# Layer 0's MLP in two phases, with sums in PSUM and activations through DRAM, in a two-layer encoder on one Trainium2 core

## The chip, the cores and the metric

The kernel runs as one program on one core of a Trainium2 chip. The metric is device time in microseconds (us) of that core. Three executions of the kernel before took 2149.87, 2150.5 and 2151.79 us, median 2150.5.

## The reference

256 tokens of width 2048 pass two layers. Each layer is modulated by a vector `c`; the part that matters here is the MLP:

```
for l in range(2):
    mod = silu(c) @ w_ada[l] + b_ada[l]          # six vectors of 2048: sh_a, sc_a, g_a, sh_m, sc_m, g_m
    h = rmsnorm(x) * (1 + sc_a) + sh_a
    ...                                          # two kinds of attention, x += g_a * mix
    h = rmsnorm(x) * (1 + sc_m) + sh_m
    y = square(relu(h @ w_mlp_in[l])) @ w_mlp_out[l]     # 2048 -> 8192 -> 2048
    x = x + g_m * y
return rmsnorm(x, final_norm_g)
```

All is float32. The products with weights are computed with each operand in two reduced-precision parts, high and low ("hi", "lo"): hi by hi, hi by lo and lo by hi.

## The kernel before, in words

**Weights.** `weights` (L167, L170) loads 1 MB by SyncE (SP) into one of five `raw` buffers; ScalarE (ACT) copies the hi part, VectorE (DVE) subtracts for the lo part, each in two halves of 1024 columns. Four hi and four lo halves fit. A `raw` buffer is free again when its lo is done. SP issues its transfers in one order that is fixed when the program is built; the order on each engine comes from a planner, except that TensorE in the MLPs keeps program order (`manual_schedule`).

**Ada.** The product `silu(c) @ w_ada` does not go to TensorE. Each of its 192 blocks is a 1 MB load into a `raw` buffer and one DVE multiply with a running sum (L323; one block of the 192 goes another way). The blocks are spread over the kernel: each call of `weights` earns a credit of `self.rate`, and each whole credit issues one ada load, whose DVE product is placed behind the splits of a later call. `ada_need` forces what is not there in time. When a pair of blocks is summed, its two columns of `mod` are written (L334, L336).

**First product of the MLP.** `wides` takes two tiles of 128 of the 8192 columns at a time: for 16 slices of the width, hi weights stand in TensorE and the hi and lo activations pass (512 columns, L232), then the lo weights and hi activations (256 columns, L235). In layer 0 the first 12 tiles are computed while the norm is applied, so 52 tiles, 26 pairs, are left for `mlp`.

**Second product, layer 0 (`mlp`).** The 8192 columns are taken in four blocks of 2048. After 16 tiles of a block, `rows` (L1325, L1327, L1329) multiplies them: the activations stand, 512 columns of weights pass, three matmuls for each of 16 slices, two token halves and four groups of 512 output columns. Each block's sums leave PSUM: copied for the first block, added to `y` by DVE for the other three (L1025). In the last block the output groups are finished one after the other, `turned` transposes finished ones and adds them to `x`, and `ahead` starts layer 1's input product.

**Second product, layer 1 (`mlp_last`).** The 8192 columns are 32 pairs of tiles. Output columns 0 to 1023 are summed in PSUM over all 32 pairs while the first product still runs (phase 1, four pairs behind it). A pair's activations, 2 by 2 blocks with the 2 by 2 blocks of its weights, can be multiplied in eight block products of three matmuls, 24 matmuls (`eight`), or in seven (`products`, 21 matmuls), after additions on the weights (`seven_weights`, L1155 to L1166) and on the activations (`sums4`). The parts of the activations (28 pairs) and of their sums are written to DRAM (`spill`) and read again (`fetch`, the tile `back`). Phase 2 then does output columns 1024 to 2047 for the first 24 pairs (13 by `eight`, 11 by `products`), and `rows` does the last 8 pairs in two groups of 512 columns (`c` = 2, 3). `leave` copies the seven-product banks out (L1215) and `gather` adds them up.

**The end.** `end_tile` finishes 512 output columns of a token half: times `g_m` (L1279), plus `x` (L1280), square with row sum (L1265), times the norm's weight; for the last group the root and reciprocal follow, and `end` scales the rows (L1299, L1301, L1303) and writes them out (L1307).

**Pools.** The activations `h`, `hid`, `y` and `back` share one pool `up` of 40 tiles of 256 KB; the additions' hi and lo parts in `seven_weights` have a pool `kp` that exists in layer 1's MLP only; PSUM has eight banks.

Of the kernel before, what the change touches and what calls it, by code (L numbers as in the profile page):

```python
# [26 lines left out]
NFB = DFF // D  # L27
# [73 lines left out]
ORDER = 1, 2, 3, 5, 7, 6, 4  # L101

# [3 lines left out]
RATE_A0, RATE_Q, RATE_A3, RATE_O, RATE_A1, RATE_A2, RATE_K, RATE_M, RATE_V = 0.7, 2.7, 1.7, 0.75, 0.5, 0.7, 0.6, 0.68, 1.4  # L106
# [3 lines left out]
class Trunk:  # L110
    def __init__(self, ctx, tc, io):
# [4 lines left out]
        self.up = pool("up", 40)  # L116
# [7 lines left out]
        self.ap = self.late.enter_context(tc.tile_pool(name="ap", bufs=6))  # L124
# [20 lines left out]
    def u(self, name, dt=F32):  # L145
        return self.up.tile([P, 2, T], dt, tag="u", name=self.name(name))
# [40 lines left out]
    def parts(self, name):  # L187

        v = self.u(name, F32R)
        return v[:, 0], v[:, 1], v.rearrange("p a b -> p (a b)")  # L190
# [125 lines left out]
    def ada_sums(self, after=None):  # L316
# [4 lines left out]
        for w, l, g, i in now:  # L321
            acc = self.macc[l, g]
            ins = nc.vector.scalar_tensor_tensor(  # L323
                w, w, 1.0, self.cond, ALU.mult, ALU.mult, accum_out=acc[:, i : i + 1]
            )
            self.summed = ins
            if after is not None:
                self.follow(ins, after)
            if i % 2:
                c = slice(i - 1, i + 1)  # L330
                v = V_BADA + 96 * l + NK * g + i
                b = self.vec[:, v - 1 : v + 1]
# [20 lines left out]
    def ada_need(self, l, g, i, after=None):  # L353
        most = self.most
# [279 lines left out]
    def ahead_rest(self, st, first, acc, after, loads=0):  # L634

        h = []
        for p in range(first, 8):
# [7 lines left out]
            if p >= after:  # L645
                upto = NK if p == 7 else 2 * (p - after + 1)
                while len(h) < upto:
                    h += self.modulated(r, len(h), self.mod[st.l, st.sh], self.mod[st.l, st.sc], after=self.lo)
# [13 lines left out]
    def modulated(self, r, k, sh, sc, whole=None, after=None, scaled=False):  # L662
# [3 lines left out]
        out = [self.parts("h") for _ in range(2)]  # L666
# [45 lines left out]
    def norm_then_by_k(self, l, acc, sh, sc, src, n, nwhole, fill=(), early=()):  # L712
# [5 lines left out]
        for p in range(8):  # L718
# [10 lines left out]
            h += self.modulated(of, k, self.mod[l, sh], self.mod[l, sc], whole, self.lo if p - 1 in early else None, not sh or p == 0)  # L729
# [26 lines left out]
    def layer(self, l, acc, st):  # L756
# [190 lines left out]
        with self.tc.manual_schedule(engines={mybir.EngineType.PE}) if l else nullcontext():  # L947
# [23 lines left out]
            else:  # L971
                h, banks = self.norm_then_by_k(l, acc, 3, 4, io["w_n0"], 3, 0)
                high = self.high
                first = NNORM, lambda: [
                    self.relu2(b, after=a) for b, a in zip(banks, [high, *self.highs, *self.highs[1:] * 3])
                ]
# [4 lines left out]
    def mlp(self, l, h, first, g):  # L981
        io = self.io
        done, leave = first
        y = [[None] * 4 for _ in range(2)]
        acc = None
        nxt = self.ahead(l + 1, 0, 1, io["w_a1"][0])
        held = []
        for fb in range(NFB):
            hid = []
            for m in range(0 if fb else done, NK, 2):  # L990
                pss = self.wides([io["w_m1"][l, NK * fb + m + j - NAHEAD] for j in range(2)], h)
                if leave:
                    hid += sum(leave(), [])
                    leave = None
                    held = [pss]
                    continue
                for ps in held + [pss]:
                    hid += self.relu2(self.joined(ps, self.t("sum")))
                held = []
            last = fb == NFB - 1  # L1000
            for cols in ((0, 1), (2,), (3,)) if last else ((0, 1), (2, 3)):
                n = len(cols)
                todo = ()
                if last:
                    self.ada_need(l, 5, NK - 1)
                    todo = (0, 1) if cols == (2,) else (2,) if cols == (3,) else ()
                pss = [[self.bank("py") for _ in range(2)] for _ in cols]
                steps = 8 * n // 2
                for kp in range(steps):
                    w = self.weights(io["w_m2"][l, fb, cols[0] // 2, (cols[0] % 2) * 4 + kp])  # L1010
                    self.rows(pss, w, hid[kp * NK // steps : (kp + 1) * NK // steps], kp == 0, kp == steps - 1)
                    if todo and kp == 1:
                        for c in todo:
                            acc = self.turned(c, y, g, acc, nxt)
                if cols == (3,):
                    self.rate = 0.0
                    self.ahead_step(nxt, 0)
                for c, ps in zip(cols, pss):
                    for t in range(2):
                        flat = ps[t].rearrange("p a b -> p (a b)")  # L1020
                        if fb == 0:
                            y[t][c] = self.u("y").rearrange("p a b -> p (a b)")
                            self.nc.scalar.activation(y[t][c], flat, AF.Copy)
                        else:
                            self.nc.vector.tensor_tensor(y[t][c], flat, y[t][c], ALU.add)  # L1025
        acc = self.turned(3, y, g, acc, nxt)
        return self.ahead_rest(nxt, 1, acc, 2, 7), nxt

    def mlp_last(self, l, h, first, g):
        io, tc = self.io, self.tc  # L1030
        done, leave = first
        self.ada_need(l, 5, NK - 1)
        self.late.close()
        self.kp = self.late.enter_context(tc.tile_pool(name="kp", bufs=1))
        self.dp = self.late.enter_context(tc.tile_pool(name="dp", bufs=1, space=bass.MemoryType.DRAM))
        hid, part, kept = {}, {}, {}
        sevens = range(3, NSPLIT, 2)
# [3 lines left out]
        def own(j, v, bias=None):  # L1041
            hid[j] = self.hidden(v, bias)
            if j < NPAIR - LAG:
                kept[j] = self.spill(hid[j], f"a{j}")

        def sums(j, v):
            part[j] = self.sums4(v)
            if j in sevens:
                kept[j] += self.spill(part[j], f"s{j}")

        for j in range(lead, NPAIR):
            pre = [self.t("pre") for _ in range(2)]
            step = j - LAG
            for i in range(2):
# [12 lines left out]
                if i == 0:  # L1067
                    banks = banks or {p: self.flat(self.bank("p7")) for p in ORDER}
                    w = self.seven_weights(io["w_s"][0, step])
# [4 lines left out]
        for j in range(NPAIR - LAG, NPAIR):  # L1074
            if (NPAIR - j) % 2:
                self.products(banks, ORDER, self.seven_weights(io["w_s"][0, j]), hid[j], part[j], False, j == NPAIR - 1)
            else:
                self.eight(banks, self.weights(io["w_s"][0, j]), hid[j], (0,) if j == NPAIR - LAG else (), j == NPAIR - 2)
        first = self.leave(banks)
        banks = {p: self.flat(self.bank("p8")) for p in (0, *ORDER)}  # L1080
        for j in range(NSPLIT):
            if j == 4:
                y = self.gather(first)
            a = self.fetch(kept[j][:2])
            if j in sevens:
                p = self.fetch(kept[j][2:])
                self.products(banks, ORDER, self.seven_weights(io["w_s"][1, j]), a, p, j == 3, j == NSPLIT - 1, (2, 3, 4))
            else:
                self.eight(banks, self.weights(io["w_s"][1, j]), a, (0, 2, 3, 4) if j == 0 else (), j == NSPLIT - 2)
        y = [a + b for a, b in zip(y, self.gather(self.leave(banks)))]  # L1090
        late, hid = hid, []
        for j in range(NSPLIT, NPAIR):
            hi, lo = self.fetch(kept[j]) if j in kept else late[j]
            hid += [(hi[:, i], lo[:, i], None) for i in range(2)]
        rows, turn, done = self.end_plan(y, g)
        work = {2: {1: [rows(2)], 2: [rows(3), turn(2)], 3: [turn(3)]}, 3: {0: [rows(0), rows(1)], 1: [turn(0), done(0)], 2: [turn(1), done(1)]}}
        for c in (2, 3):
            pss = [[self.bank("py") for _ in range(2)]]
            for kp in range(4):
                w = self.weights(io["w_e"][0, c - 2, kp])  # L1100
                self.rows(pss, w, hid[kp * 4 : kp * 4 + 4], kp == 0, kp == 3, c == 3 and kp == 3)
                for f in work[c].get(kp, ()):
                    f()
            for t in range(2):
                self.before = self.end_tile(y[t][c], self.flat(pss[0][t]), c, t)
        return y, None

# [3 lines left out]
    def hidden(self, v, bias=None):  # L1111

        nc = self.nc
        r = v
        if bias is None:
            nc.scalar.activation(r, v, AF.Relu)
# [4 lines left out]
        return self.both(r, self.u("hidl", F32R), "hidh")  # L1121

    def sums4(self, r):
# [6 lines left out]
        return self.both(s.rearrange("p (a b) c -> p a (b c)", a=2), self.u("suml", F32R), "sumh")  # L1130
# [55 lines left out]
    def eight(self, banks, w, a, first, last):  # L1186
# [3 lines left out]
        for p, t, c in ((0, 1, 1), (2, 0, 0), (3, 0, 1), (4, 1, 0)):  # L1190
            for k in range(2):
                self.product(banks[p], x(k, t), n(k, c), p in first and k == 0, last and p == 0 and k == 1)
# [25 lines left out]
    def end_plan(self, y, g):  # L1218
# [30 lines left out]
        def done(c):  # L1249
            def f():  # L1250
                for t in range(2):
                    self.end_square(y[t][c], c, t)
# [10 lines left out]
    def end_square(self, z, c, t):  # L1263
        sq = self.flat(self.t("zsq"))
        self.nc.scalar.activation(sq, z, AF.Square, accum_out=self.part[:, c, t : t + 1])  # L1265
# [6 lines left out]
    def end_tile(self, z, ps, c, t):  # L1272

        nc = self.nc
        flat = lambda v: v.rearrange("p a b -> p (a b)")
        m, zf = flat(self.t("zm")), z
        if c == 3 and t == 0:
            zf = self.y3 = flat(self.u("zf"))
        nc.vector.tensor_tensor(m, ps, self.gb[c], ALU.mult)  # L1279
        last = nc.vector.tensor_tensor(z, m, z, ALU.add)  # L1280
        self.end_square(z, c, t)
        if c < 3 or t == 0:
# [405 lines left out]
```

## Time and profile before

| | |
|---|---|
| median of three executions | 2150.5 us |
| profiled execution, its own time | 2150.3 us |
| its span in the profile | 2148.5 us |
| mean granted clock of TensorE | 0.997 |
| HBM read, written | 602.81 MB, 22.54 MB |

How to read it: lines L... are those of the kernel before. A row of a group gives line, engine, operation, output tile <- input tiles, shapes and count, then the busy time in us, the mean of one in ns, and the idle time of the engine ahead of it with what ended it. "PE" is a matmul, "PEld" a weight load that overlaps it. Matmuls overlap, so the duration of one (about 390 ns for 512 columns) is more than the distance from one to the next. The chain is the sequence of work that ended last, followed back from the end. In layer 0's MLP the first `wides` begins at 474.9 us and the last matmul of `rows` at 1114 us; layer 1's phase 2 is about 1967 to 2090 us.

### The profile page before, as it was taken

The page shows a single profiled execution, that of the slowest core. Times are in us where ns is not written, and L with a number is a line of the kernel's source. Part 1 is how long each engine was busy: PE and PEld are TensorE (multiplying, and loading weights), DVE is VectorE, ACT ScalarE, POOL GpSimd, SP SyncE. Part 2 cuts the span into 40 slices and gives each one's busy share as a digit, 9 for nine tenths or more (in the row PEclk, how much of TensorE's full clock was granted, in tenths as well). Part 3 has the DMA queues.
Part 4 walks back from the last instruction along what each step waited for, and adds up shares of the span by engine and source line. Part 5 has one row for each costly group of instructions (what it writes and reads, how often), then busy time and mean ns, then how long its engine had stood idle before and what let it go on. Part 6 is the DMA issues. An engine that isn't in the chain of part 4 may idle for free.

```text
span 2148.5 us, 30886 instructions
## 1 busy us (share of the span) xinstructions
PE 2127.4 (99%) x11925; PEld 1866.4 (87%) x11925; DVE 1809.8 (84%) x2336; ACT 1244.1 (58%) x1937; POOL 24.7 (1%) x43
## 2 busy tenths in 40 slices
PE   8999999999999999999999999999999999999998
PEld 6899888998888888888889898989888888888886
DVE  8999988888687778778798788798998888888887
ACT  6555664555455355345447656647767666665554
POOL 0000000000000000000001000000000000000000
PEclk9999999999999999999999999999999999999999
DMA  9987988799888888888877657786776766758993
GB/s 399 424 329 263 342 331 291 264 377 332 320 319 325 332 296 337 328 309 318 333 251 259 249 198 294 274 299 208 268 268 237 263 250 231 263 193 303 356 332 115
DMA packets 108006, 627.38 MB, mean 292 GB/s; under 512 B 11985, under 2 KB 11985, under 8 KB 41809
## 3 DMA queue, kind: packets, MB, share of 16 engines
q1 hardware_dynamic: 107570, 624.75, 77.7%
q8 instruction: 94, 1.54, 0.3%
q10 hardware_dynamic: 288, 0.66, 0.1%
q14 instruction: 54, 0.44, 0.1%
HBM read 602.81 MB, written 22.54 MB: 291 GB/s over the span
## 4 chain that ended last, share of the span: by engine, by line
PE 92%; DVE 3%; ACT 3%; DMA 2%; issue 0%; DVEq 0%; ACTq 0%
PE ps L232 24%; PE ps L235 13%; PE py L1327 6%; PE py L1325 6%; PE py L1329 6%; PE p L1174 4%; PE p L1175 4%; PE p L1176 4%; PE pk L262 3%; PE pk L210 2%; PE pk L208 2%; PE pk L209 2%; PE pv L276 1%; PE pv L278 1%; PE pv L277 1%; DVE lo L170 1%
## 5 line engine op out<-in xcount | busy, mean ns | idle before, releaser
L170 DVE TENSOR_TENSOR lo<-raw,hi 128x1024 fp32r<-128x1024 f32 (+1 forms) x638 | 746.1, 1190 | 222.3 <-ACT hi L167 152.3
L167 ACT ACTIVATE hi<-raw 128x1024 fp32r<-128x1024 f32 (+1 forms) x638 | 645.3, 1031 | 448.5 <-PE py L1329 186.1
L232 PE MATMUL ps<-h,hi 128*128 128x512 f32 x2016 | 475.1, 390 | 0.0
L232 PEld LDWEIGHTS ps<-h,hi 128*128 128x128 f32 x2016 | 376.3, 188 | 77.0 <-ACT hi L167 0.2
L323 DVE SCALAR_TENSOR_TENSOR ada<-ada,cond 128x2048 f32<-128x2048 f32 x191 | 434.7, 2283 | 3.1 <-DMA ada<-in_w_ada 2.9
L235 PEld LDWEIGHTS ps<-h,lo 128*128 128x128 f32 x2016 | 254.2, 191 | 7.6 <-DVE lo L170 0.4
L235 PE MATMUL ps<-h,lo 128*128 128x256 f32 x2016 | 256.6, 283 | 0.2 <-DVE lo L170 0.2
L1325 PE MATMUL py<-hi,hid 128*128 128x512 f32 x512 | 163.0, 390 | 0.0
L1327 PE MATMUL py<-lo,hid 128*128 128x512 f32 x512 | 163.0, 389 | 0.0
L1329 PE MATMUL py<-hi,hid 128*128 128x512 f32 x512 | 162.9, 389 | 0.0
L1327 PEld LDWEIGHTS py<-lo,hid 128*128 128x128 f32 x512 | 96.1, 188 | 20.3 <-DVE lo L170 0.4
L1329 PEld LDWEIGHTS py<-hi,hid 128*128 128x128 f32 x512 | 96.1, 188 | 20.0
L1325 PEld LDWEIGHTS py<-hi,hid 128*128 128x128 f32 x512 | 95.8, 188 | 19.6
L1166 DVE TENSOR_TENSOR ul<-u,uh 128x2048 fp32r<-128x2048 f32 x41 | 93.9, 2291 | 15.5 <-ACT uh L1165 12.8
L1165 ACT ACTIVATE dh<-raw 128x1024 fp32r<-128x1024 f32 x82 | 65.1, 841 | 67.4 <-PE p L1176 57.2
L1060 ACT ACTIVATE pre<-ps 128x256 f32<-128x256 f32 x116 | 37.9, 379 | 101.4 <-PE ps L235 101.4
L1165 ACT ACTIVATE uh<-u 128x1024 fp32r<-128x1024 f32 x82 | 85.7, 1055 | 11.8 <-issue 10.5
L208 PE MATMUL pk<-h,hi 128*128 128x256 f32 x304 | 85.4, 287 | 2.2 <-ACT h L673 1.5
L209 PE MATMUL pk<-h,hi 128*128 128x256 f32 x304 | 86.2, 286 | 0.0
L210 PE MATMUL pk<-h,lo 128*128 128x256 f32 x304 | 85.2, 287 | 0.3 <-DVE lo L170 0.2
L1166 DVE TENSOR_TENSOR dl<-raw,dh 128x1536 fp32r<-128x1536 f32 x41 | 71.8, 1752 | 6.6 <-ACT dh L1165 6.6
L262 PE MATMUL pk<-hf,w 128*128 128x256 f32 x288 | 63.1, 379 | 0.0
(393 smaller groups left out, 3830.2 us busy)
## 6 DMA issues: line engine op xcount, KB each, us to landing
ada<-in_w_ada SPq DMA_DIRECT2D x191, 1024.0 KB, 5.2
raw<-in_w_m SPq DMA_DIRECT2D x174, 1024.0 KB, 5.6
raw<-in_w_s SPq DMA_DIRECT2D x56, 1024.0 KB, 6.4
raw<-in_w_ob SPq DMA_DIRECT2D x24, 1024.0 KB, 5.0
raw<-in_w_dv SPq DMA_DIRECT2D x16, 1024.0 KB, 5.2
raw<-in_w_q SPq DMA_DIRECT2D x16, 1024.0 KB, 5.0
back<-a SPq DMA_DIRECT2D x56, 256.0 KB, 6.8
raw<-in_w_n SPq DMA_DIRECT2D x16, 768.0 KB, 5.9
```

The source lines that it names most:

```text
L167: ins = self.high = nc.scalar.activation(hi, v, AF.Copy)
L170: ins = nc.vector.tensor_tensor(lo, v, hi.bitcast(F32), ALU.subtract)
L208: mm(ps, hi, x[0], start=first, stop=False, skip_group_check=shared)
L209: mm(ps, hi, x[1], start=False, stop=False, skip_group_check=shared)
L232: mm(ps.rearrange("p a b -> p (a b)"), part(w, 0, k), both, start=k == 0, stop=False)
L235: mm(ps[:, 0], part(w, 1, k), x, start=False, stop=k == nk - 1)
L323: ins = nc.vector.scalar_tensor_tensor(w, w, 1.0, self.cond, ALU.mult, ALU.mult, accum_out=acc[:, i : i + 1])
L1165: nc.scalar.activation(hi[:, c:m], v[:, c:m], AF.Copy)
L1166: nc.vector.tensor_tensor(lo, v, hi.bitcast(F32), ALU.subtract)
L1325: mm(o, xh[:, tok], hi[:, part[j]], start=start, stop=False)
L1327: mm(o, xh[:, tok], lo[:, part[j]], start=False, stop=False)
L1329: mm(o, xl[:, tok], hi[:, part[j]], start=False, stop=stop)
```

## The change

Layer 0's `mlp` takes the form of layer 1's, with one difference: its phase 1 uses `eight` alone, so that the four sums for columns 0 to 1023 take four banks and two pairs of `wides` fit beside them. Each round of phase 1 is one pair of `wides` and one plain step (two in the three rounds behind the first). Phase 2 is shared by both layers (`second`): steps 3, 5, ... 23 by `products`, the others by `eight`. The last 8 pairs go through `rows` with single groups of 512 columns.

The pool `up` shrinks from 40 to 32 tiles; 8 tiles of a pool `xp` hold the later half of the attention's `h`, layer 0's first four activations and the sums. `kp` for layer 0 takes the place of `xp` and of the pool of `ahead` while phase 2 runs. Rates: `RATE_M` 0.68 to 0.76, `RATE_A1` 0.5 to 0.6, `RATE_A2` 0.7 to 0.9, new `RATE_S` 0.2 for phase 2 and `RATE_E` 0.75 for the last 8 pairs. `mod` is written for eight blocks at once, except layer 0's shifts and scales.

At the end of layer 1, the last group's later two weight loads are multiplied for token half 0 first, then half 1; of half 1, the last load's sums go to two banks of 256 columns each, which are finished one after the other, and the norm's weight is multiplied in ahead of the reciprocal.

```diff
     def mlp(self, l, h, first, g):
...
+        for j in range(lead, NPAIR):
+            pss = self.wides([io["w_m1"][l, 2 * j + i - NAHEAD] for i in range(2)], h)
+            if j == lead:
+                for k, (ps, after) in enumerate(leave()):
+                    own(k, ps, r=self.t("relu"), after=after, far=k < 4)
+            pre = [self.t("pre") for _ in range(2)]
+            for i, ps in enumerate(pss):
+                for k in range(2):
+                    nc.scalar.activation(pre[k][:, i], ps[:, k], AF.Copy)
+            nc.vector.tensor_tensor(pre[0], pre[0], pre[1], ALU.add)
+            own(j, pre[0])
+            for _ in range(2 if j > lead else 0):
+                if step <= j - LAG:
+                    banks = banks or {p: self.flat(self.bank("p4")) for p in PLAIN}
+                    self.eight(banks, self.weights(io["w_s"][2 * l, step]), hid[step], PLAIN if step == 0 else (), ())
+                    step += 1
+        for j in range(step, NPAIR):
+            self.eight(banks, self.weights(io["w_s"][2 * l, j]), hid[j], (), PLAIN if j == NPAIR - 1 else ())
+        self.rate = RATE_S
...
+        banks = self.second(l, kept)
+        for t, v in enumerate(self.gather(self.leave(banks))):
+            y[t][2:] = v
...
+        hid = self.rest(hid, kept)
+        self.rate = RATE_E
...
+        for c in (2, 3):
+            ps = [self.bank("py") for _ in range(2)]
+            for kp in range(4):
+                w = self.weights(io["w_e"][l, c - 2, kp])
+                self.rows([ps], w, hid[4 * kp : 4 * kp + 4], kp == 0, kp == 3)
...
+    def second(self, l, kept, then=None):
+        banks = {p: self.flat(self.bank("p8")) for p in (*PLAIN, *(p for p in ORDER if p not in PLAIN))}
+        for j in range(NSPLIT):
+            if then is not None and j == 4:
+                then()
+            a = self.fetch(kept[j][:2])
+            w = self.io["w_s"][2 * l + 1, j]
+            if j in SEVENS:
+                p = self.fetch(kept[j][2:])
+                self.products(banks, ORDER, self.seven_weights(w), a, p, j == SEVENS[0], j == SEVENS[-1], PLAIN)
+            else:
+                self.eight(banks, self.weights(w), a, PLAIN if j == 0 else (), (0,) if j == NSPLIT - 2 else ())
+        return banks
...
     def mlp_last(self, l, h, first, g):
...
+        for t in range(2):
+            for n, (x, w) in enumerate(ws if t == 0 else ws[:4]):
+                self.product(ps[t], self.token(x, t), w, False, n == (3 if t else 7))
+            if t == 0:
+                self.end_last(y[0][3], ps[:1], 0, (slice(0, 512),))
+                continue
+            self.end_add(y[1][3], ps[1], 3)
+            halves = slice(0, 256), slice(256, 512)
+            ps = [self.flat(self.bank("pz")) for _ in halves]
+            for p, c in zip(ps, halves):
+                for n, (x, w) in enumerate(ws[4:]):
+                    self.product(p[:, c], self.token(x, t), [z[:, c] for z in w], n == 0, n == 3)
+            self.end_last(y[1][3], ps, 1, halves)
...
+    def end_last(self, z, ps, t, cols):
+        m = self.flat(self.u("zf"))
+        some = self.some[:, t : t + 1]
+        for i, c in enumerate(cols):
+            self.end_add(z, ps[i], 3, c)          # times g_m, plus z
+            sq = self.s("zq", 1)
+            self.end_square(z[:, c], sq)
+            nc.vector.tensor_tensor(m[:, c], z[:, c], self.fgb[3][:, c], ALU.mult)
...
+        r = self.s("rt", 1)
+        nc.scalar.activation(r, sq, AF.Sqrt, bias=some, scale=INV_D)
+        nc.vector.reciprocal(r, r)
```

More of the change, by code (lines that the diff above doesn't have):

```diff
@@ L981, in mlp @@
     def mlp(self, l, h, first, g):
-        io = self.io
+        io, nc = self.io, self.nc
         done, leave = first
-        y = [[None] * 4 for _ in range(2)]
-        acc = None
[L986 to L1004, printed above, removed]
-                    self.ada_need(l, 5, NK - 1)
[L1006 to L1025, printed above, removed]
@@ new lines, in mlp, with own @@
+        nxt = self.ahead(l + 1, 0, 1, io["w_a1"][0])
+        hid, kept = {}, {}
+        lead, step, banks = done // 2, 0, None
+        def own(j, v, **k):
+            hid[j] = self.hidden(v, **k)
+            if j < NPAIR - LAG:
+                kept[j] = self.spill(hid[j], f"a{l}{j}")
+            if j in SEVENS:
+                kept[j] += self.spill(self.sums4(k.get("r", v)), f"s{l}{j}")
+        for j in range(lead, NPAIR):
[14 more added lines that the diff above has]
+                    step += 1
@@ L1029, in mlp_last, with rest @@
+    def rest(self, hid, kept):
+        out = []
+        for j in range(NSPLIT, NPAIR):
+            hi, lo = self.fetch(kept[j]) if j in kept else hid[j]
+            out += [(hi[:, i], lo[:, i], None) for i in range(2)]
+        return out
     def mlp_last(self, l, h, first, g):
@@ L1079, in mlp_last @@
         first = self.leave(banks)
[L1080 to L1089, printed above, removed]
+        y = []
@@ L1090, in mlp_last @@
+        banks = self.second(l, kept, lambda: y.extend(self.gather(first)))
         y = [a + b for a, b in zip(y, self.gather(self.leave(banks)))]
[L1091 to L1094, printed above, removed]
+        hid = self.rest(hid, kept)
         rows, turn, done = self.end_plan(y, g)
-        work = {2: {1: [rows(2)], 2: [rows(3), turn(2)], 3: [turn(3)]}, 3: {0: [rows(0), rows(1)], 1: [turn(0), done(0)], 2: [turn(1), done(1)]}}
+        work = {2: {1: [rows(2)], 2: [rows(3), turn(2)], 3: [turn(3)]}, 3: {0: [rows(0), rows(1), turn(0), done(0)], 1: [turn(1), done(1)]}}
@@ L1191, in eight @@
             for k in range(2):
-                self.product(banks[p], x(k, t), n(k, c), p in first and k == 0, last and p == 0 and k == 1)
+                self.product(banks[p], x(k, t), n(k, c), p in first and k == 0, p in last and k == 1)
     def leave(self, banks):
@@ L1369, in joined @@
         return out
-    def relu2(self, ps, bias=None, after=None):
-        r = self.t("relu")
-        if bias is None:
-            ins = self.nc.scalar.activation(r, ps, AF.Relu)
-            if after is not None:
-                self.follow(ins, after)
-        else:
-            for i in range(2):
-                self.nc.scalar.activation(r[:, i], ps[:, i], AF.Relu, bias=bias[:, i : i + 1])
-        self.nc.scalar.activation(r, r, AF.Square)
-        return self.split(r, "hid", True)
     def rope_k(self, ps, l):
```

174 lines of the change are left out of this document (93 added, 81 removed).

## The prediction

> **What bounds the kernel now.** I read the page's busy table first, then the chain in layer 0's MLP, then windows by stage, then the groups.
>
> ```profile
> span 2148.5 us, 30886 instructions
> PE 2127.4 (99%) x11925; PEld 1866.4 (87%) x11925; DVE 1809.8 (84%) x2336; ACT 1244.1 (58%) x1937; POOL 24.7 (1%) x43
> ```
> TensorE is busy almost always, but a busy PE need not be at its peak, so I take its pitch. First the chain across one change from the first product to the second in layer 0 (start, us, what):
> ```profile
> 661.92 7.28 PE ps L232 x32
> 669.20 3.83 PE ps L235 x32
> 673.04 0.47 PE py L1325 x2
> ```
> A pair of first-product tiles takes 7.28 + 3.83 = 11.11 us, a 256-column matmul 3.83/32 = 0.120, and the second product starts without a gap. The pitch of a 512-column matmul, from the end of layer 1's second phase (48 matmuls from the first row to the second):
> ```profile
> 2079.61 0.39 PE L1174 MATMUL p<-uh,back 128*128 128x512 f32 x1
> ...
> 2090.27 0.39 PE L1176 MATMUL p<-uh,back 128*128 128x512 f32 x1
> ```
> (2090.27 - 2079.61)/47 = 0.227 us. Layer 0's second product:
> ```profile
> L1325 PE MATMUL py<-hi,hid 128*128 128x512 f32 x512 | 163.0, 390 | 0.0
> ```
> L1327 and L1329 have as many: 1536. 26 pairs by 11.11 plus 1536 by 0.227 is 288.9 + 348.4 = 637 us. So here matmuls removed are time removed, while what feeds TensorE keeps up. What feeds it, by windows (PE, PEld, DVE, ACT, POOL busy, clock, DMA share, GB/s):
> ```profile
> 584.00:760.00 176.00, 176.00 (x898) 150.88 (x897) 138.52 (x157) 89.01 (x116) 6.55 (x6) 1.00 0.86 323
> 1518.00:1700.00 182.00, 182.00 (x976) 157.86 (x975) 164.03 (x183) 125.74 (x188) 0.00 (x0) 1.00 0.68 254
> 1966.00:2090.00 124.00, 124.00 (x547) 102.35 (x546) 102.51 (x88) 66.69 (x78) 0.00 (x0) 1.00 0.94 355
> 60.00:70.00 10.00, 10.00 (x48) 8.59 (x47) 9.05 (x15) 7.08 (x14) 0.00 (x0) 1.00 1.03 427
> 1970.00:1980.00 10.00, 10.00 (x46) 8.28 (x45) 9.83 (x11) 4.71 (x5) 0.00 (x0) 1.00 1.04 408
> ```
> First row: layer 0's MLP now (DVE 79%, 323 GB/s). Second and third: layer 1's two phases, the form that layer 0 is to take; TensorE stands still in neither, with DVE at 90% or DMA at 355 GB/s. The last two: the DMA engines saturated, 427 GB/s with loads alone, 408 with small fetches among them.
>
> **The change, step by step.**
>
> *Second product.* Phase 1 gives columns 0 to 1023 to 32 plain steps of 24 matmuls (768, as before). Phase 2 has 13 plain steps and 11 of 21, 543; the rest 8 loads of 24, 192. Sum 1503, 33 fewer: 33 by 0.227 = 7.5 us, on the path. First product, transposes and the lead into layer 1 keep their counts.
>
> *DVE.* Per split and ada product of layer 0, and per step of layer 1:
> ```profile
> L170 DVE TENSOR_TENSOR lo<-raw,hi 128x1024 fp32r<-128x1024 f32 x231 | 277.1, 1220 | 120.2 <-ACT hi L167 75.2 <-issue 22.1 <-PE ps L235 17.3
> L323 DVE SCALAR_TENSOR_TENSOR ada<-ada,cond 128x2048 f32<-128x2048 f32 x79 | 180.3, 2282 | 0.0
> L202 DVE TENSOR_TENSOR hid<-relu,hid 128x256 fp32r<-128x256 f32 x64 | 24.0, 418 | 5.4 <-ACT hid L201 5.4
> L1366 DVE TENSOR_TENSOR sum<-ps,sum 128x256 f32<-128x256 f32 x52 | 21.5, 417 | 0.0
> ```
> ```profile
> L1166 DVE TENSOR_TENSOR ul<-u,uh 128x2048 fp32r<-128x2048 f32 x40 | 91.6, 2291 | 14.9 <-ACT uh L1165 12.2
> L1166 DVE TENSOR_TENSOR dl<-raw,dh 128x1536 fp32r<-128x1536 f32 x40 | 70.1, 1751 | 6.6 <-ACT dh L1165 6.6
> L1155 DVE TENSOR_TENSOR u<-raw 128x1024 f32<-128x1024 f32 x40 | 48.7, 1217 | 1.2 <-DMA raw<-in_w_s 1.2
> L1157 DVE TENSOR_TENSOR u<-u,raw 128x512 f32<-128x512 f32 x40 | 27.6, 690 | 1.1
> L1156 DVE TENSOR_TENSOR u<-u,raw 128x512 f32<-128x512 f32 x40 | 27.4, 685 | 0.3
> L1416 DVE TENSOR_TENSOR suml<-sum,sumh 128x512 fp32r<-128x512 f32 x29 | 19.9, 685 | 0.2
> L1416 DVE TENSOR_TENSOR hidl<-pre,hidh 128x512 fp32r<-128x512 f32 x28 | 19.1, 684 | 0.4 <-ACT hidh L1415 0.4
> ```
> A seven-product weight costs DVE 6.6 us against 2.4 for two plain splits, per step of 21 by 0.227 = 4.8 us. Phase 2 sums to 13 by 2.4 + 11 by 6.6 = 104 us and 2.6 ada products (13 loads at rate 0.2) 6: 110 of its 123 us, 90%. In phase 1 one round (a pair and a plain step, 11.11 + 5.44 = 16.6 us) has six splits 7.3, 2.28 ada products 5.3, joining and splitting the activation 1.4, and sums in 11 of 26 rounds about 0.7: 14.7 us, 89%. Both are at what layer 1 bears unharmed, so I cost them at nothing; cover gone, phase 2's 6 us of ada is the price. ACT trades 256-wide copies for 512-wide ones and splits the combined weights; it is busy 89 of 176 us now and would have to double to be seen. The mod sums go out in eights instead of pairs, fewer small DVE operations: idle time either way.
>
> *DMA, all on SP's queue.* Weights stay 116 loads. Ada loads go from 79 (the count above) to 84 by 0.76 + 13 by 0.2 + 8 by 0.75 = 72; the 7 left go to layer 1's attention, whose rates rise (17 loads by 0.1 and 16 by 0.2 more, 5) and whose last ada is due when its MLP begins; one or two loads forced there would cost 2.3 us of DVE each (the L323 row), beside TensorE's first products. New are spills and fetches, as in layer 1 (out<-in, KB each, us to landing; a weight load, then the fetches):
> ```profile
> raw<-in_w_s SPq DMA_DIRECT2D x56, 1024.0 KB, 6.4
> ```
> ```profile
> back<-a SPq DMA_DIRECT2D x49, 256.0 KB, 6.9
> back<-s SPq DMA_DIRECT2D x22, 256.0 KB, 6.2
> ```
> Written are 28 pairs and 11 sums by 0.52 MB, 20.4 MB, and as much read. With 188 loads of 1.05 MB the MLP moves 238 MB in 632 us: 377 GB/s, phase 1 379, phase 2 375, against 323 now. That lies between the 355 that ran with a DMA share of 0.94 and the 408 of saturation; nearer to neither. I take it as borne, because what is served at 408 is the same mix, and keep the other end for the range. A spill that waits for its activation holds the weight loads behind it on SP; the five raw buffers cover it, and layer 1 issues the same order.
>
> The Trainium skill, "DMA: Bandwidth & Descriptors", section "Where 436 GB/s comes from", has HBM traffic bound by about 358 GB/s per core, and its measured single-core load near 425. By the former, an estimate, the MLP would need 238/358 = 665 us, 33 more; the 427 row above speaks for the latter.
>
> *The junction in each round.* Both forms of weights share four hi and four lo buffers. A pair takes all four lo; the plain step behind it needs its two lo 0.2 and 0.9 us after the pair ends at 11.1, and their buffers come free at 7.28 + 0.96 = 8.2 and 9.2 us. Before, this stood four times in the MLP, now in 25 rounds. DVE there, before:
> ```profile
> 670.25 2.36 DVE L170 TENSOR_TENSOR lo<-raw,hi 128x1024 fp32r<-128x1024 f32 x2 [2.99 <-issue]
> ```
> The two splits end at 672.61, 0.4 us before the pair does and 1.3 before the second would be needed, after idle time that a DVE at 89% won't always have. An ada product of 2.3 us begun just before 8.2 ends at 10.5 and puts the splits to 11.7 and 12.9, 0.4 and 0.9 us late: the price is 0 to 25 by 0.9 = 22 us. The junctions of before cost 0, and the order on DVE must fall badly for the other end; near the lower one I take 0.05 each, +1.3 us.
>
> *Pools and banks.* The activation pool falls from 40 to 32 with 8 apart; at the worst (16 h, 6 pairs of activations) 28 are live, so nothing waits that did not. Between the phases of layer 0 four banks are copied out by ACT:
> ```profile
> L1215 ACT ACTIVATE y<-p 128x512 f32<-128x512 f32 x16 | 8.8, 603 | 2.7 <-PE p L1176 2.5
> ```
> Phase 2 starts on the banks of the finished first product and asks for the copied ones in its fourth step, 3 by 5.4 = 16 us later, against 4 by 0.6 = 2.4 us: nothing, and 2.4 us if the cover is gone. Its combined weights overlay the far pool, whose last user is step 23's sums, eight steps before.
>
> *The end.* The last matmul, and what follows it on DVE, the chain (zsq, final product) and SP:
> ```profile
> 2139.21 0.39 PE L1329 MATMUL py<-hi,hidl 128*128 128x512 f32 x1
> ```
> ```profile
> 2139.63 0.69 DVE L1279 TENSOR_TENSOR zm<-py,gb 128x512 f32<-128x512 f32 x1
> 2140.36 0.69 DVE L1280 TENSOR_TENSOR y<-zm,y 128x512 f32<-128x512 f32 x1
> ```
> ```profile
> 2141.08 0.73 ACT zsq L1265 x2
> ...
> 2143.24 0.66 DVE y L1301
> ```
> ```profile
> 2142.61 2.51 SPq L1307 DMA_DIRECT2D out_y<-y  x4
> ```
> From 2139.6 to the end are 8.9 us. On half the width zm and y take 0.42 each (L1366), 0.54 less, the square about 0.2 less, and the last product becomes a plain scaling of 0.48 (2143.24's row has 0.66): about 0.9. SP now issues four outputs in a burst and its last leaves at 2145.12, 1.2 after the last product; after, token half 0's four go out while half 1 still multiplies, so up to 1 us more. PE pays 24 by 0.120 for 12 by 0.227: +0.15. I take -1.7 net, bounds -2.6 and +0.5 (half 0's scalings ahead of half 1 on DVE).
>
> **Sum**, on the profiled execution's 2150.3 us (0.2 below the median 2150.5): 2150.3 - 7.5 - 1.7 + 1.3 = 2142.4.
>
> **Rivals.** *A, DMA becomes the bound in layer 0's MLP* (slower): loads land late in SP's order, an ada product waits on DVE and the splits behind it with it. It decides where the sustained rate falls under 238/(632 + 9) = 371 GB/s; at 365 the MLP takes 652, 20 more: 2150.3 - 9.2 + 20 = 2161. For it: 355 at share 0.94 makes 378 a full share, and 89% DVE at once; against: 408 and 427. 17%. The page's 358 is its far end.
> *B, the junction costs 0.35 us in each round* (no change): +8.8 in place of 1.3, 2150. For it the 1.3 us of margin, less than one ada product; against, the gapless ones of before. 13%.
> *C, phase 2's ada and one handover show*, 4 us beyond the forecast: 2146. For it 110 of 123 us on DVE; against, layer 1's phase 2 without a gap. 8%.
>
> **How the numbers follow.** Forecast 62%, own range 2139 to 2146. 0.2%, about what a measurement here tells from no change, is 4.3 us. Faster: the forecast and half of C, 0.66; same: the rest of C and most of B, 0.16; slower: A and some of B, 0.18. The range runs from 2139.5 (tail's best, no junction loss) to 2154, into A.
>
> **What would show it.** 33 fewer 512-column matmuls in the MLP; each round 16.6 us long; PE idle under 2 us there; DMA 370 to 380 GB/s; the end 7 us behind the last matmul. Wrong if a round's plain step begins late behind lo (B), if DVE's ada shows idle time on DMA (A), or if phase 2 takes over 125 us (C).

## The result, and the profile after

The changed kernel takes 2210.1 us (median of four, 2204.3 to 2216.5) for 2150.2 (four, 2147.7 to 2151.8) in the same session: a ratio of 1.028, 95% interval 1.0245 to 1.0316. It is slower by 60 us where 8 us less were forecast. The profiled execution took 2205.9. Its page:

```profile
span 2204.1 us, 31205 instructions
PE 2139.4 (97%) x11904; PEld 1863.3 (85%) x11904; DVE 1857.2 (84%) x2302; ACT 1273.8 (58%) x1996; POOL 18.2 (1%) x43
```

TensorE has fewer matmuls than before (11904 for 11925) and is idle for 65 us instead of 21. Where: the first and last matmul of layer 1's input product (`pa`) frame the stages, first of the kernel before, then of the changed one, with the changed one's second phase (`back`, first start) beside it.

```profile
L209 PE MATMUL pa<-al,hi x192: 277/282/295, 1114.9 to 1489.9; 128*128 128x258 f32 x192
```
```profile
L213 PE MATMUL pa<-al,hi x192: 277/282/419, 1164.3 to 1545.3; 128*128 128x258 f32 x192
```
```profile
L1227 PE MATMUL p<-hi,back x208: 389/389/397, 991.9 to 2141.5; 128*128 128x512 f32 x104
```

Up to the end of layer 0's MLP 49.4 us are lost, in layer 1's attention 381.0 - 375.0 = 6.0, from there to the end 0.2. The MLP by windows (columns as in the prediction), before and after:

```profile
474.00:981.00 507.00, 507.00 (x2571) 434.05 (x2570) 399.37 (x454) 257.52 (x341) 6.55 (x6) 1.00 0.86 323
```
```profile
474.00:981.00 507.00, 468.95 (x2385) 392.87 (x2384) 383.31 (x398) 254.19 (x370) 0.00 (x0) 0.98 0.88 341
981.00:1104.00 123.00, 123.00 (x544) 101.72 (x543) 104.30 (x88) 67.07 (x74) 0.00 (x0) 1.00 0.99 382
```

The loss is in phase 1: from 474 to 991.9, 518 us where 26 pairs by 11.11 and 768 matmuls by 0.227 make 463. TensorE is idle there, the DMA engines move 341 GB/s of the 379 needed, and no engine is full. Phase 2 runs as forecast, at 382 GB/s. What TensorE waited for in phase 1 (us in total, times, longest), and what SP's queue waited for at its head:

```profile
PE ps L236 <- ACT hi L171: 20.5, 9, 8.4
PE p L1228 <- DVE lo L174: 11.3, 17, 0.8
PE p L1227 <- ACT hi L171: 5.6, 5, 1.7
```
```profile
SPq L1189 <- ACT hidh L1466: 171.8, 22, 10.1
```

L1189 is `spill`. One such wait in SP's order of time (start, duration, issue):

```profile
687.20 0.43 SPq L188 DMA_DIRECT2D raw<-in_w_m  x1
687.72 0.58 SPq L317 DMA_DIRECT2D ada<-in_w_ada  x1
696.34 0.33 SPq L1189 DMA_DIRECT2D a<-hidh  x1
698.30 0.33 SPq L1189 DMA_DIRECT2D a<-hidl  x1
698.72 0.38 SPq L188 DMA_DIRECT2D raw<-in_w_m  x1
```

For 8 us nothing is issued; the next pair's second load (698.72) stands behind a spill that waits for the pair now being multiplied. At the end of that pair, ACT:

```profile
690.19 0.66 ACT L1007 ACTIVATE pre<-ps 128x256 f32<-128x256 f32 x2 [6.06 <-PE ps L239]
691.40 1.06 ACT L171 ACTIVATE hi<-raw 128x1024 fp32r<-128x1024 f32 x1 [0.55 <-DMA raw<-in_w_s]
692.37 0.64 ACT L1007 ACTIVATE pre<-ps 128x256 f32<-128x256 f32 x2
692.89 1.06 ACT L171 ACTIVATE hi<-raw 128x1024 fp32r<-128x1024 f32 x1
```

The plain step's first hi stands behind the first tile's two copies and waits for its load, the second behind all four copies. So hi and lo are late when the pair has ended: here TensorE stops 0.44 us for hi and 0.76 and 0.78 us for lo, the kind of stop in the second and third row of its waits. The order on ACT is not the same in every round; one round earlier only two copies stand ahead of the second hi.

### The profile page after: what moved, and what is told of

Same layout as the page of the kernel before. It is cut to its first block, busy times and chain, and to the rows that moved or that the text cites. A ratio compares the mean times of both kernels' runs of the same rounds, so it can differ in the third digit from the quotient of the medians.

```text
span 2204.1 us, 31205 instructions
## 1 busy us (share of the span) xinstructions
PE 2139.4 (97%) x11904; PEld 1863.3 (85%) x11904; DVE 1857.2 (84%) x2302; ACT 1273.8 (58%) x1996; POOL 18.2 (1%) x43
## 4 chain that ended last, share of the span: by engine, by line
PE 79%; DVE 9%; DMA 5%; ACT 5%; issue 2%; SPq 0%; DVEq 0%; ACTq 0%
PE ps L236 21%; PE ps L239 11%; PE p L1228 8%; PE p L1229 8%; PE p L1227 8%; DVE lo L174 3%; PE pk L266 3%; DVE ada L327 3%; DMA raw<-in_w_m 2%; ACT hi L171 2%; PE pv L281 1%; PE pv L282 1%; PE pv L280 1%; PE pk L212 1%; PE pk L213 1%
## 5 line engine op out<-in xcount | busy, mean ns | idle before, releaser
L174 DVE TENSOR_TENSOR lo<-raw,hi 128x1024 fp32r<-128x1024 f32 (+1 forms) x616 | 719.0, 1190 | 204.0 <-ACT hi L171 158.4
L171 ACT ACTIVATE hi<-raw 128x1024 fp32r<-128x1024 f32 (+1 forms) x616 | 617.5, 1029 | 358.6 <-DMA raw<-in_w_m 51.2
L1219 DVE TENSOR_TENSOR ul<-u,uh 128x2048 fp32r<-128x2048 f32 x52 | 119.2, 2292 | 27.2 <-ACT uh L1218 24.6
L1218 ACT ACTIVATE uh<-u 128x1024 fp32r<-128x1024 f32 x104 | 109.0, 1057 | 43.2 <-DVE u L1210 18.5
L1228 PE MATMUL p<-lo,hidh 128*128 128x512 f32 x272 | 109.9, 404 | 11.9 <-DVE lo L174 11.3
L1227 PE MATMUL p<-hi,hidh 128*128 128x512 f32 x272 | 108.3, 398 | 5.6 <-ACT hi L171 5.6
L1229 PE MATMUL p<-hi,hidl 128*128 128x512 f32 x272 | 107.2, 394 | 0.0
L1104 ACT ACTIVATE pre<-ps 128x256 f32<-128x256 f32 x116 | 37.9, 379 | 100.5 <-PE ps L239 100.4
L1007 ACT ACTIVATE pre<-ps 128x256 f32<-128x256 f32 x104 | 34.3, 380 | 99.1 <-PE ps L239 99.0
L1229 PE MATMUL p<-hi,back 128*128 128x512 f32 x208 | 81.0, 389 | 0.0
L1228 PE MATMUL p<-lo,back 128*128 128x512 f32 x208 | 80.9, 389 | 0.0
L1227 PE MATMUL p<-hi,back 128*128 128x512 f32 x208 | 80.9, 389 | 0.0
```

Of the source, the lines that this page charges most:

```text
L171: ins = self.high = nc.scalar.activation(hi, v, AF.Copy)
L174: ins = nc.vector.tensor_tensor(lo, v, hi.bitcast(F32), ALU.subtract)
L1218: nc.scalar.activation(hi[:, c:m], v[:, c:m], AF.Copy)
L1219: nc.vector.tensor_tensor(lo, v, hi.bitcast(F32), ALU.subtract)
L1227: mm(ps, x[0], w[0], start=first, stop=False)
L1228: mm(ps, x[0], w[1], start=False, stop=False)
```

## The experiments

Three theories. ORDER: a spill that waits at the head of SP's queue holds the loads behind it. BYTES: the DMA engines can't carry phase 1 (rival A). JUNCTION: the plain step's lo is late behind each pair (rival B). Times of single runs unless said; the kernel before took 2148 to 2155 beside them. The changed kernel's own four runs lie up to 12 us apart, so a smaller difference from it is no evidence by itself.

**Spills on GpSimd's queue**
```
-            self.nc.sync.dma_start(d, v.bitcast(F32))
+            q = self.nc.gpsimd if name[1] == '0' else self.nc.sync
+            q.dma_start(d, v.bitcast(F32))
```


> Layer 0's spills are issued by GpSimd's queue in place of SP's; bytes, waits and everything else as in the changed kernel. Theory ORDER (a spill waits at the head of SP's queue for its activations and the weight loads behind it start late): phase 1 of layer 0 goes from 518 us to under 475, the run to 2146-2162 us. Theory BYTES (the DMA engines cannot carry weights, ada, spills at once): phase 1 stays over 505, the run at 2200-2216. Theory JUNCTION (DVE's lo splits are late behind each pair): the matmuls' waits for DVE's lo of 11 us stay and the run stays over 2195.

2161.3 us, 45 less, as ORDER has it. Window of phase 1 (it ends at 945.6) and TensorE's waits in it:
```profile
474.00:945.00 471.00, 465.20 (x2422) 399.51 (x2421) 384.81 (x402) 256.36 (x374) 40.11 (x74) 0.99 0.97 374
```
```profile
PE ps L236 <- ACT hi L171: 5.1, 2, 3.4
PE p L1229 <- DVE lo L174: 0.5, 2, 0.3
```
The same bytes at 374 GB/s, so BYTES is out. But two things have changed: the planner, which orders the engines when the program is built, now puts the plain step's two hi ahead of the pair's copies:
```profile
678.77 2.01 ACT L171 ACTIVATE hi<-raw 128x1024 fp32r<-128x1024 f32 x2 [0.45 <-DMA raw<-in_w_s]
684.49 0.66 ACT L1007 ACTIVATE pre<-ps 128x256 f32<-128x256 f32 x2 [3.71 <-PE ps L239]
686.41 0.66 ACT L1007 ACTIVATE pre<-ps 128x256 f32<-128x256 f32 x2 [1.26 <-PE ps L239]
```

**Spills on SP that are ready at once** (they write a slice of `x`, not the activation)
```
+            v = self.x[:, 2 * i : 2 * i + 2] if name[1] == '0' else v.bitcast(F32)
```


> Layer 0's spills stay on SP and keep their number and bytes, but write a slice of x, which is ready long before, in place of the activations (what phase 2 reads back of layer 0 is therefore not the activations). ORDER: no spill waits, phase 1 under 475 us, the run 2146-2162. BYTES: the same bytes, phase 1 over 505, the run 2200-2216. JUNCTION: over 2195.

2189.9, outside all the forecasts. SP has no spill waits left, but ACT's order is the late one and TensorE waits 19 times, 12.7 us, for lo. ORDER alone doesn't carry the 55 us.

**Spills a sixteenth in size, in their places on SP** (the other columns are not written)
```
+                self.nc.sync.dma_start(d, v[:, :, :16].bitcast(F32))
```


> Layer 0's spills keep their waits and their places on SP but write 16 of 256 columns, a sixteenth of the bytes (only the first pair is written whole, and phase 2 reads that pair for all). ORDER: the loads are held as before, phase 1 500-518 us, the run 2190-2206. BYTES: 20 MB less in phase 1, so it falls under 480 and the run to 2146-2170. JUNCTION: over 2195.

2199.4, as ORDER has it: without 15/16 of the bytes it is 6.5 us less, within the spread of the changed kernel, and SP still waits 176.6 us for `hidh`. A second answer against BYTES.

**Each spill issued one round later in the program**
```
-                kept[j] = self.spill(hid[j], f"a{l}{j}")
+                wait.append((j, hid[j], f"a{l}{j}"))     # issued behind the next pair's loads
```


> Layer 0's spills stay on SP, but each is issued one round later in the program, behind the next round's pair. ORDER: most waits at SP's head vanish, phase 1 465-490 us, the run 2150-2178. BYTES: phase 1 over 505, the run 2200-2216. JUNCTION: over 2195.

2206.8, no gain. The waits for `hidh` fell to 30.6 us, those for `sumh` are 29.6, and waits for a free `raw` buffer rose from 61 and 17 us to 130 and 70; TensorE waits 22 times for lo. A miss.

**The plain step's weights requested ahead of the pair's copies, spills on SP**
```
+            ws = [self.weights(io["w_s"][2 * l, step + i]) for i in range(n)]
             pre = [self.t("pre") for _ in range(2)]
```


> The changed kernel, with the plain step's two weights requested in the program ahead of the pair's activation copies and spill in each of layer 0's rounds; the spills stay on SP. So on SP two loads go out before each waiting spill, and on ACT and DVE the weights' hi and lo come before the copies that wait for the end of the pair. JUNCTION in its new form (the second hi stands behind two copies that wait for the pair, 0.7 us a round in 25 rounds, and the clock lost after each of those stops): 16 to 25 us less than the changed kernel's 2206, 2181 to 2190, and the waits of the plain step's products for lo go to nearly 0. ORDER alone (a spill that waits for its activation holds whatever loads stand behind it, wherever they stand): the pair's loads of the next round are still behind the spill, so most of the loss stays, 2195 to 2206. If both are cured by this order alone: 2155 to 2170.

2207.9, no gain: the planner mixed both orders over the rounds, and the spills kept their place ahead of the next pair's loads.

**ACT's order forced, three ways.** First, GpSimd spills with the plain step's second hi behind all four copies (in every round; in the changed kernel two or four copies stand ahead of it, so that the expectation's "as it stands" is too kind):
```
+                    copied = nc.scalar.activation(pre[k][:, i], ps[:, k], AF.Copy)
...
+                    self.eight(banks, self.weights(io["w_s"][2 * l, step], after=copied, first=1), ...)
```


> Spills on GpSimd's queue (2161.3 us), and on ACT the second hi of every plain step in layer 0's first phase is put behind the pair's four copies, as it stands in the changed kernel. JUNCTION: each round's plain step then waits for lo, 0.5 to 0.9 us in 25 rounds, and the clock is lost behind each stop as in the kernel with ready spills: 2161 + 12 to 28 = 2173 to 2189. ORDER alone: within 4 us of 2161, since the loads come as early as before.

2253.1, 92 us more: far beyond either forecast. One round of TensorE:
```profile
714.61 0.39 PE L1230 MATMUL p<-hi,hidl 128*128 128x512 f32 x1
716.00 0.49 PE L1228 MATMUL p<-hi,hidh 128*128 128x512 f32 x1 [1.00 <-ACT hi L171]
717.26 0.50 PE L1229 MATMUL p<-lo,hidh 128*128 128x512 f32 x1 [0.77 <-DVE lo L174]
...
718.60 0.63 PE L1228 MATMUL p<-hi,hidh 128*128 128x512 f32 x1
719.03 0.63 PE L1229 MATMUL p<-lo,hidh 128*128 128x512 f32 x1
...
721.59 0.51 PE L1229 MATMUL p<-lo,hidh 128*128 128x512 f32 x1
```
```profile
594.69:602.69 8.00, 7.23 (x31) 5.76 (x32) 8.00 (x12) 5.94 (x8) 1.62 (x3) 1.00 0.74 224
716.00:724.00 8.00, 7.24 (x24) 5.55 (x24) 7.20 (x10) 4.34 (x6) 1.08 (x2) 0.79 0.75 270
718.60:721.60 3.00, 3.00 (x9) 2.31 (x8) 3.00 (x6) 0.80 (x2) 0.83 (x2) 0.50 0.81 337
754.00:794.00 40.00, 36.47 (x170) 29.83 (x169) 28.37 (x30) 17.48 (x26) 3.25 (x6) 0.91 0.80 297
```
The two stops lose 1.39 + 1.26 - 2 by 0.227 = 2.2 us. Then seven matmuls from 718.60 take (721.59 - 718.60)/7 = 0.427 us each instead of 0.227, with the granted clock at 0.50: another 1.6 us or so. The two stops come in all 25 rounds, the low clock in the last 20 of them; in the first five (the row from 594.69 is the fifth) the same stops leave it at 1.00. 25 by 2.2 + 20 by 1.6 = 87 of the 92 us. The prediction bounded the junction's price by the wait alone; with the clock it is 3.9 us a round. The Trainium skill, "TensorE: Matmul & The Clock Gate", section "HAM oscillation — how this bites in real kernels", has the clock halved by idle gaps of over 3.4 us; here gaps of 1.2 and 1.0 us, 1.3 apart, were followed by it in 20 of 25 rounds. What decides whether a stop is followed by it stays open: in the changed kernel the three stops at 692 us were not (clock 1.00 from 696 to 700), while those at 616 to 619 were (0.61 from 620 to 624).

Second, ready spills on SP (the slice of `x`) with both hi forced ahead of the second tile's copies, and third, the changed kernel with the same:
```
+                    if ws and i == 1:
+                        self.follow(ins, self.high)
```


> Spills on SP that are ready when they are issued (a slice of x, 2189.9 us), with the plain step's two hi put ahead of the second tile's copies on ACT. JUNCTION: the 12.7 us of waiting for lo and about 10 us of lower clock behind it go, 2162 to 2172. If what is left there is SP's own order (loads behind loads that wait for a buffer), it stays at 2182 to 2192.

> The changed kernel (2206) with waiting spills on SP and ACT's early order forced. JUNCTION as the larger cause: 2178 to 2190. ORDER as the one that ends last (the late loads hold hi and lo back whatever ACT's order is): 2196 to 2208. If both are additive, the gain is what the first run of this call loses.

2170.1, in JUNCTION's forecast, and 2198.6, in ORDER's. Together (us):

| spills | late order on ACT | early order |
|---|---|---|
| on SP, waiting | 2205.9 | 2198.6 |
| on SP, ready | 2189.9 | 2170.1 |
| on GpSimd | 2253.1 (further back) | 2161.3 |

Without the waits on SP the early order is worth 20 us (2189.9 - 2170.1), and the waits for lo fall from 12.7 us to 1.3. With the waits in place the 7 us are within the changed kernel's spread, and the forced order helps less: both hi come ahead of the second tile's copies, but in many rounds behind the first tile's, and 19 waits for lo (7.6 us) are left. Taking the waits away alone gives 16 us (2205.9 - 2189.9), both together 36. So both are causes, and they do not simply add. That GpSimd is another 9 us faster than ready spills on SP is not explained by these runs.

**Why layer 1 bears the same order.** The changed kernel's layer 1, from 1580 to 2010: SP's waits, the window, and the loads (KB, us to landing):
```profile
SPq L1189 <- ACT hidh L1466: 204.7, 23, 9.4
```
```profile
1580.00:2010.00 430.00, 430.00 (x2293) 372.52 (x2292) 381.15 (x413) 287.58 (x435) 0.00 (x0) 1.00 0.65 245
```
```profile
raw<-in_w_m SPq DMA_DIRECT2D x51, 1024.0 KB, 6.2
raw<-in_w_s SPq DMA_DIRECT2D x32, 1024.0 KB, 6.7
```
The spills wait there even longer, and TensorE for nothing. The difference is 245 GB/s, a load each 430/83 = 5.2 us. So the test is layer 0 with fewer loads: `RATE_M` 0.3 for 0.76, nothing else.

> The changed kernel with the rate of adaptive blocks in layer 0's first phase at 0.3 a load for 0.76: some 39 blocks of 1.05 MB fewer there, about 290 GB/s for 379 worked out, and 2.3 us of VectorE less for each. Read is the first phase alone (the first product pair at 474 us to the second phase's first matmul; 518 us in the changed kernel, 463 worked out), since the blocks come back later. If a wait at the head of SP's queue hurts only where the loads can't catch up: 465 to 485 us. If each wait delays TensorE whatever the load: 505 to 520. If ACT's late order is enough by itself: 490 to 505.

Phase 1 ends at 945.0 for 991.9, 471 us (the whole kernel takes 2245, as the ada blocks come back later). Window, SP's and TensorE's waits:
```profile
474.00:945.00 471.00, 466.36 (x2423) 400.24 (x2423) 304.81 (x323) 270.24 (x378) 0.00 (x0) 0.99 0.80 293
```
```profile
SPq L1189 <- ACT hidh L1466: 69.1, 24, 11.5
```
```profile
PE p L1228 <- DVE lo L174: 2.8, 5, 0.8
PE ps L236 <- ACT hi L171: 1.7, 1, 1.7
```
Spills that wait at the same places in SP's order, and phase 1 is as short as with the spills on GpSimd (471.6): the wait hurts where the loads have no time in hand. ACT's order is the early one here, its four copies in a row, so the run to set beside it is the changed kernel with the early order forced and all its loads: 509.5 us (474 to 983.5). (VectorE has less to do here too; that it isn't VectorE shows in the GpSimd kernel, as busy as the changed one.) An estimate of the time in hand: five buffers by the time per load, less 6.4 us to land and 2.4 for the splits. Phase 1 needs 5.28 loads in 16.6 us, 3.1 each: 15.7 - 8.8 = 7 us, against waits of 171.8/22 = 7.8, up to 10.1. Layer 1 has 26 - 8.8 = 17 against 8.9; at the rate 0.3 it is 3.9 loads a round, 12 against 2.9. By this estimate phase 1 is short by little on average; its long waits are what the cover plainly misses.

**The rest of the loss, on the GpSimd kernel.** Ada blocks taken earlier in layer 1's attention (`RATE_A1` 1.0 for 0.6, `RATE_A2` 0.7 for 0.9); and the first four activations back in the main pool (`far=k < 4` removed):

> Spills on GpSimd's queue (2161.3 us, its last sums of layer 1 begin 11.2 us later than in the kernel before), and layer 1's attention takes its last adaptive-weight products earlier: rate 1.0 for 0.6 in its first stage of outputs, 0.7 for 0.9 in the next. If the seven displaced products are what layer 1's start lost, the 5 to 6.6 us behind 1520 us shrink to 0 to 2: 2155 to 2157.5. If that loss is of another kind (fetches, the clock), the time stays within 1 us of 2161. If the earlier products only move the collision, layer 1's attention loses what its MLP gains, and the time stays too, with the shift already there at the keys and values of layer 1.

> Spills on GpSimd's queue (2161.3 us), and the first four activations of layer 0 take the main pool's buffers instead of the eight set apart, so that the first sums find theirs free at once. If the eight buffers are what stops TensorE between 485 and 524 us (its first phase takes 472.6 us for 463 worked out), that stage takes 463 to 467 us: 2152 to 2157. If the stop at the start is the first weights landing late or the low clock, whatever buffers are used, the time stays within 1.5 us of 2161.

2157.9 and 2155.7, 3.4 and 5.6 us less, each in its forecast or 0.4 beside it. Differences of this size between single runs mean little alone; the stages bear them out: layer 1's attention takes 376.8 us for 381.9 in the first, phase 1 465.9 for 471.6 in the second. The displaced ada shows in the changed kernel's DVE, where `lo` for layer 1's input product stands behind it, and in TensorE's waits:
```profile
1527.27 2.29 DVE L327 SCALAR_TENSOR_TENSOR ada<-ada,cond 128x2048 f32<-128x2048 f32 x1 [0.20 <-DMA ada<-in_w_ada]
...
1530.28 1.82 DVE L174 TENSOR_TENSOR lo<-raw,hi 128x768 fp32r<-128x768 f32 x2
```
```profile
PE pa L214 <- DVE lo L174: 3.3, 1, 3.3
```

**All four together** (GpSimd, weights first, main pool, ada earlier):

> All together: spills on GpSimd's queue, the plain step's weights requested ahead of the pair's copies, the first four activations in the main pool, layer 1's last adaptive products taken earlier. If the four causes named are all there are, the forecast's sum is left, 2150.3 - 7.5 - 1.7 = 2141 with up to 5 us for what the junction and the start still cost: 2141 to 2147. If the DMA engines are the bound behind it all (BYTES), it stays at 2155 to 2161 with a DMA share of 1.00.

2153.6, between the two forecasts. What was left: a stop of TensorE at 1093 us, in the last eight loads of layer 0's MLP, with DVE full:
```profile
1092.00:1096.00 4.00, 1.75 (x8) 1.15 (x7) 4.00 (x6) 2.00 (x3) 0.00 (x0) 1.00 0.72 297
1096.00:1100.00 4.00, 4.00 (x13) 3.10 (x12) 4.00 (x4) 0.28 (x1) 0.00 (x0) 0.57 0.63 209
```
2.2 us of standing, then four at a clock of 0.57. So three rates were changed (`RATE_E` 0.4 for 0.75, `RATE_A1` 0.8, `RATE_A2` 0.9), and the same was run with the spills on ScalarE's queue:

> The kernel with the four cures (2153.6 us), with three rates changed so that fewer adaptive products fall where it still lost: 0.4 a load for 0.75 in layer 0's last eight loads (there VectorE was busy 4.00 of every 4 us from 1068 to 1096 and TensorE then stood 2.2 us for lo, with the granted clock at 0.57 in the 4 us behind), 0.8 for 1.0 in layer 1's first outputs (1.8 us of waiting at 1200 us) and 0.9 for 0.7 in its last. If the products displaced onto a full VectorE are what is left, both stops go, with the clock they cost, 4 + 3 us: 2146 to 2149. If the DMA engines or the tail are, it stays at 2152 to 2155. If the displaced products must be forced ahead of layer 1's MLP, 2155 or more.

> The same kernel with layer 0's spills issued by ScalarE in place of GpSimd. ScalarE makes hidh itself, but waits for VectorE's hidl before the second half can go: if any waiting issue holds up what stands behind it on its engine, ScalarE's copies of the next pair and its hi splits come late, and the time is 2155 to 2180, with TensorE waiting for hi. If only SP's loads suffer from such a wait, it equals the GpSimd version within 2 us.

2149.0 and 2161.5, each in its first forecast. On ScalarE's queue TensorE stands longer for hi (its largest stop 9.6 us for 3.3): a wait on an issue costs whatever stands behind it on that engine. On GpSimd the spills wait too (282.6 us), with nothing but spills behind them in phase 1:
```profile
POOL a L1191 <- ACT hidh L1468: 282.6, 22, 18.9
```

**The best version** (`RATE_A1` 0.9), **and the same with the end as before:**

> The 2149.0 us kernel with the rate of adaptive products in layer 1's first outputs at 0.9 for 0.8, so that none is left to be forced behind 1470 us: its one at 1480 us cost 3.3 us of waiting ahead of layer 1's MLP and the clock behind it. If that is what is left of the displaced products, 2144.5 to 2147, faster than before by 0.15 to 0.3%. If the earlier products bring back the wait at 1200 us (1.8 us in the kernel with rate 1.0), 2147 to 2150, no difference that counts.

> The same kernel with the end as before: the last block whole, not in halves. The difference of the two is the tail's price: by the prediction the halves save 1.7 us (-0.5 to 2.6), by the traces so far the kernels with halves end 8.1 us behind their last matmul for 8.9 before, so that the old end should cost 0.5 to 1.2 us more. If the tail is worth nothing, the two agree within 0.3 us.

Eleven runs each, 21 of the kernel before (2148.9): 2150.1, ratio 1.0004 (0.9995 to 1.0013), no difference, where 2144.5 to 2147 was forecast; and 2150.8, ratio 1.001 (1.0001 to 1.0019). The first's profiled execution was its fastest (2146.3):
```profile
474.00:939.00 465.00, 462.45 (x2424) 398.02 (x2423) 384.71 (x402) 256.10 (x375) 39.95 (x74) 1.00 0.98 380
```
```profile
L213 PE MATMUL pa<-al,hi x192: 277/282/295, 1108.7 to 1486.6; 128*128 128x258 f32 x192
```
In it layer 0 gains 1114.9 - 1108.7 = 6.2 us, layer 1's attention gives back 377.9 - 375.0 = 2.9, the end gains 0.7. This sets the fastest of eleven beside a run of the kernel before (2150.3) that would be among the slowest of the 21 (2146.9 to 2150.9), so it shows where the time went, not a gain. Other runs of it reach 2153.2; what sets that spread of 7 us (4 before) isn't settled.

The last matmuls of the two ends, halves (span 2144.5) and whole (span 2146.5):
```profile
2136.09 0.28 PE L1231 MATMUL pz<-hi,hidl 128*128 128x256 f32 x1
```
```profile
2137.49 0.39 PE L1369 MATMUL py<-hi,hidl 128*128 128x512 f32 x1
```
8.4 and 9.0 us from the last matmul's start to the end of the span.

## Why the prediction was wrong, step by step

- **The step that failed:** "A spill that waits for its activation holds the weight loads behind it on SP; the five raw buffers cover it, and layer 1 issues the same order". The mechanism was named and costed at nothing. The cover was 7 us by the estimate above, the wait 7.8 on average and up to 10.1. And layer 1 was no evidence, as it needs 245 GB/s. Taking the spills off SP returned 45 of the 56 us lost, 46 of them in phase 1, ACT's early order included; taking only the waits away returned 16. No rival of the prediction has this wait.
- **The junction**, taken as 0.05 us a round with bounds of 0 and 0.9: 17 waits of 0.66 in the changed kernel. What decided was not an ada product on DVE, as rival B had it, but the second hi's place on ACT, which the prediction did not look at ("busy 89 of 176 us now and would have to double to be seen"): busy time says nothing of order. And two such stops can cost 1.6 us of clock beside their length, so the upper bound was too low by far: 3.9 us a round in 20 of 25 rounds when forced.
- **Rival A** gave a time on the right side for the wrong reason. DMA did run short, at 341 GB/s, but by issue and not by rate: 374 to 382 were carried in three kernels. The Trainium skill, "DMA: Bandwidth & Descriptors", section "Where 436 GB/s comes from", has about 358 GB/s per core for HBM beside a measured load of 425; the traces go beyond the first.
- **"So nothing waits that did not"** of the pools: wrong, by 5.6 us with the spills on GpSimd; the first sums wait for one of the eight tiles set apart, held until its spill has landed.
- **The displaced ada**, "one or two loads forced there would cost 2.3 us of DVE each": right in kind, and 6.0 us in size, of which 5.1 came back with the earlier ada.
- **Rival C:** right in kind (DVE full beside the rest's ada, a stop of 2.2 us), in the eight loads behind phase 2, not in it.
- **Right:** 33 fewer matmuls (phase 2 took 123.5 us, 991.9 to 1115.4, for 543 by 0.227 = 123.3), the DMA rate in phase 2, DVE there (85% for 90). With the causes taken away, layer 0's MLP is 6.2 us shorter in the fastest run; that this meets the forecast's 7.5 - 1.3 is partly luck, as the medians show no gain.
- **The tail**, -1.7 forecast (-2.6 to +0.5): 0.6 in the traces, 0.7 between the medians, whose intervals overlap. The end lies 8.4 us behind the last matmul, not 7. The term was too large; the sign is likely right.

## What to carry to other kernels

Before you move a transfer that waits for a result onto a queue that also issues loads, work out the queue's time in hand (buffers by the time per load, less landing and use) and set it against the wait; a stage where the same order does no harm proves nothing if its loads come further apart (here 5.2 us for 3.1). A queue with nothing behind it costs least. And look for short stops of TensorE in the order on the engine that feeds it, not in how busy that engine is, and price them at one to two times their length.

## What the runs showed of the hardware that was not expected

Two stops of about 1 us each in a round of 20 were enough to bring TensorE's pitch from 0.227 to 0.427 us for some 3 us, at a granted clock of 0.50, in 20 rounds of 25; in the other five the same stops left the clock at 1.00. And the queue that issues a transfer mattered much: the same spills took 2149.0 us from GpSimd and 2161.5 from ScalarE, and 45 us less from GpSimd than from SP, the changed order on ACT included. The Trainium skill, "DMA: Bandwidth & Descriptors", section "Issuing engines are not separate DMA queues", lets a second issuing engine save only the time to initiate a transfer; where an issue waits for data, the runs here show the wait itself to be the larger part (an issue on SP takes 0.3 to 0.6 us in the rows above, a wait there 7.8 on average).
